# Eight pre-made weight sums and four more steps by seven products in the output projection of a gated linear attention block

## The chip, the cores and the metric

The kernel runs on one core of a Trainium2 chip. The metric is the device time of one execution in microseconds (us); the time of a kernel is the median over runs of the same build on the same chip. A traced execution is shown beside it: its span runs from the first to the last instruction of the trace.

## The reference

One layer of a streaming encoder, on 256 tokens of width 2048: a chunked gated linear attention (GLA) mixer and a squared-ReLU MLP, each behind an RMSNorm, and a last RMSNorm. All of it is float32.

```
def _gla_mixer(h, w_in, w_gate_up, b_gate, o_norm, w_out):
    q, k, v, r, g_low = jnp.split(h @ w_in, [...], axis=-1)
    log_a = log_sigmoid(g_low @ w_gate_up + b_gate) / 16
    ...
    def step(state, xs):                       # over chunks of 64 tokens
        state = d_c[..., None] * state + einsum('bhck,bhcv->bhkv', k_c, v_c)
        return state, einsum('bhck,bhkv->bhcv', q_c, state)
    ...
    o = o * rsqrt(mean(o * o) + EPS) * o_norm
    return (o * silu(r)) @ w_out

def _sq_relu_mlp(h, w_up, w_down):
    a = relu(h @ w_up)
    return (a * a) @ w_down

h = h + _gla_mixer(_rmsnorm(h, gla_norm), ...)
h = h + _sq_relu_mlp(_rmsnorm(h, mlp_norm), w_up, w_down)
return _rmsnorm(h, final_norm)
```

The change concerns `(o * silu(r)) @ w_out`, a product of 256 x 2048 by 2048 x 2048, and the part of the kernel ahead of it in which the projections of `h @ w_in` and the attention are computed (the mixer).

## The kernel before

**Splits.** Float32 accuracy is reached with float32r matmuls on parts. Each weight tile is loaded raw, ScalarE (ACT) casts it to `hi` (`copy_hi`, L118), and VectorE (DVE) subtracts to `lo` (`parts`, L131; `weights`, L165). A product then takes three matmuls on TensorE (PE): hi by hi, hi by lo, lo by hi. The hi and lo tiles come in five slots each, the raw tiles in six and one more named `more`. Loads of raw tiles are issued by SyncE (SP), a few by GpSimd (POOL).

**Stages.** In the order of the trace: warm-up matmuls (L252, `WARM` pairs of records), the first natural projection (the first half of V and the gate columns, `w_vg`), the gate's work, the turned projections of K and Q (`turned`, L206, matmuls at L219), and then three natural projections (`natural`, L178, matmuls at L176) of 16 steps each, one step per 128 rows of `w_in`: natural 2 (columns from 3*KEYW, the second half of V), natural 3 (from 4*KEYW) and natural 4 (from 5*KEYW), the two halves of the output gate r. After each step but the last, `pump` takes one closure off the queue `side` and runs it: two pairs of `scores` (L517, matmuls at L523, copies at L537 and L538) during natural 2, eight calls of `attend` (L563) during natural 3. An attend multiplies the scores by V, squares on ACT (L575), scales the sum on DVE (L576), raises it to the power -1/2 on POOL (L358) and scales the result on DVE (L579), which frees the PSUM bank. This stretch, from natural 2 to natural 4, is called the mixer below.

**Output projection.** `out_group` (L713) computes 512 of the 2048 output columns; there are four groups. Each takes eight steps, in the order given by `ORDER`, one for each pair of 128 rows of `w_out` (`kp`, 0 to 7). A step is done in one of two ways: plainly, with eight products of 128 x 256 by three matmuls, or by sums, with seven products after a scheme of 2 x 2 blocks, for the pairs in `FORMED`. For a step by sums, the left operand is turned into eight forms (`turn_pair`, L611, with `form_sums`), once for all groups; the weights' four blocks are combined for every group and pair: POOL adds two blocks during a load (L744, a DMA that accumulates), DVE makes the others (`weight_sums`, L603 to L605), ACT casts the four sums (L118) and DVE subtracts for their lo (L773). Three of the seven products use the raw blocks' splits, four the sums' (`pending`, L768).

**What sets the order.** The compiler of the kernel's framework lists each engine's instructions in one order, and each engine takes them in that order. `tc.issue_after` in the code puts an instruction behind a given one in that list. DMA queues belong to the engine that issues them. The MLP behind the output projection is not touched.

Of the kernel before, what the change touches and what calls it, by code (L numbers as in the profile page):

```python
# [60 lines left out]
EVEN = (5, 6)  # L61
MR = 2 * GT
ROUNDS = HID // MR
WARM = 8
FINE = 3


# [1 line left out]
def tile_gla_mlp(ctx, tc, x, xt, cols, w_vg, w_in, w_gate, w_out, w_up, w_down, final_norm, out):  # L69
# [33 lines left out]
    def flush():  # L103
        while side:
# [101 lines left out]
    def turned(row, w, c0, even=(0,), acc=None):  # L206

        acc = acc or acc_banks(GT // P // 2)
        for kp in range(KT // 2):
            wh, wl = pair_of(w, kp, c0, even)  # L210
            for i in range(2):
                kt = 2 * kp + i
                ah, al = row(kt)
                for j in range(GT // P):
                    s = slice(j * P, (j + 1) * P)
                    o = acc[j // 2][:, j % 2 * T : (j % 2 + 1) * T]
                    for n, (u, m) in enumerate(((wh, ah), (wh, al), (wl, ah))):
# [7 lines left out]
        return acc  # L225

    HALF = [(0, 512), (512, 1024)]

# [7 lines left out]
    def rows(w, c0, n=G, r0=0):  # L236
        return lambda kt: w[r0 + kt * P : r0 + (kt + 1) * P, c0 : c0 + n]
# [365 lines left out]
    def weight_sums(u):  # L603
        nc.vector.tensor_tensor(u[:, 2], u[:, 0], u[:, 2], op=ALU.subtract)  # L604
        return nc.vector.tensor_tensor(u[:, 1::2], u[:, 1::2], u[:, 2:3].to_broadcast([P, 2, T]), op=ALU.subtract)  # L605

    FORMED = (0, 1, 7)
    in_forms = lambda a: a.rearrange("p (f s) -> p f s", f=8)
    raw_forms = [in_forms(some[:, 4:6].rearrange("p a b -> p (a b)")), in_forms(mid.tile([P, G], F32, tag="db", name="form"))]

    def turn_pair(kp, bank, gain, to):  # L611

        raw_form = raw_forms[kp == 1]
# [38 lines left out]
    def forms_o(kp):  # L652
        if kp < 2:
            return [of_pairs[:, kp, i] for i in range(2)]
        return [a[:, OFF : OFF + G].rearrange("p (f s) -> p f s", f=8) for a in (oth, otl)]

    def place_o(kt):

# [47 lines left out]
    def then_mm():  # L706
# [3 lines left out]
            yield  # L710
        last_mm[0] = newest[0]

    def out_group(g, order, summed, between):  # L713

        tt = nc.vector.tensor_tensor
        banks = [out_banks[g, t] for t in range(NT)]
        sums_banks = []
        begun = set()
        pending = None
        block = lambda i, n=1: slice(i * T, (i + n) * T)  # L720

        def product(bank, o, a, w, n, last=False):
            for x in a[: 2 - n]:
                for d in range(0, w.shape[-1], T):
                    newest[0] = nc.tensor.matmul(  # L725
                        bank[:, o + d : o + d + T], x, w[:, d : d + T],
                        start=bank in sums_banks and bank.name not in begun, stop=last, skip_group_check=True,
                    ).ins
                    begun.add(bank.name)

        def products(these, w, last=False):
            with then_mm():
                for n in range(2):
                    for bank, o, a, c in these:
                        product(bank, o, a, w[n][:, c], n, last and n == 1)

        for step, kp in enumerate(order):
            by = kp in summed
            raw = raw_tile()[:, : 2 * GT]
            src = w_out[2 * kp * P : 2 * (kp + 1) * P, g * GT : (g + 1) * GT].rearrange("(i p) c -> p i c", p=P)  # L740
            if by:
                for i in range(2):
                    last_load[0] = nc.sync.dma_start(out=raw[:, i * GT : (i + 1) * GT], in_=src[:, i])
                nc.gpsimd.dma_start(out=raw[:, :T], in_=src[:, 0, T:], accum_op=ALU.add)  # L744
            else:
                last_load[0] = nc.sync.dma_start(out=raw.rearrange("p (i c) -> p i c", i=2), in_=src)
            w = parts(raw, 2 * GT, slots(), [(T * by, 2 * GT)])
            if by:
                if not sums_banks:
                    sums_banks.extend(psum_bank(i) for i in out_ids[4:])  # L750
                f = forms_o(kp)
                at = lambda k, f=f: [a[:, k] for a in f]
                p16, p57 = sums_banks
                products([(p16, 0, at(A11), block(1)), (banks[0], T, at(A12), block(3)), (banks[0], 0, at(S4), block(2))], w)
                u = raw.rearrange("p (f s) -> p f s", f=4)
                with tc.issue_after(last_lo[0].ins):
                    weight_sums(u)
            else:
                for t, i in ((0, 0), (0, 1), (1, 0), (1, 1)):
                    products([(banks[t], 0, row_o(2 * kp + i, t), block(2 * i, 2))], w, step == len(order) - 1 and i == 1)  # L760
            if pending:
                pending()
                pending = None
            if step in between:
                with tc.issue_after(last_hi[0].ins), tc.issue_after(last_lo[0].ins), then_mm():
                    between[step]()
            if by:
                def pending(u=raw, at=at, final=kp == [k for k in order if k in summed][-1]):  # L768
                    to = slots()
                    for a in range(2):  # L770
                        copy_hi(*(x.rearrange("p (f s) -> p f s", f=4)[:, a::2] for x in (to[0][:, :G], u)))
                    with tc.issue_after(last_lo[0].ins):
                        last_lo[0] = tt(to[1][:, :G], u, to[0][:, :G].bitcast(F32), op=ALU.subtract)  # L773
# [23 lines left out]
    out_group(0, ORDER, FORMED, {  # L797
        1: lambda: (turn(on, turned_o, gain_o, 2), turn(on, turned_o, gain_o, 3, forms_o, spare_out(0))),
        3: lambda: begin_out(1),
    })  # L800
    hth, htl = (big.tile([P, KT, T], F32R, tag="A" + i, name="h" + i, bufs=1) for i in "hl")
    turned_h = lambda kt: [a[:, kt, :].rearrange("p (t s) -> p t s", t=NT) for a in (hth, htl)]
    for g in range(1, GROUPS):
        out_group(g, ORDER, FORMED, {
            1: lambda: turn(h, turned_h, g2, g - 1), 4: lambda: ssq_h(g - 1),
            **({3: lambda: begin_out(g + 1)} if g + 1 < GROUPS else {}),
        })
# [511 lines left out]
```

## Time and profile before

| | us |
|---|---|
| median of three runs | 1043.82 |
| lowest and highest run | 1043.51, 1044.12 |
| the profiled execution: its time | 1043.33 |
| the profiled execution: its span | 1041.5 |
| first matmul of warm-up to the first projection | 1.05 to 4.77 |
| mixer (natural 2 to 4) | 139.8 to 286.7 |
| output projection | 286.7 to 374.4 |
| MLP | 374.4 to about 1032 |

The granted clock of TensorE is 0.999 of full speed over the execution. In the rows of the profile, a group's line number is that of the kernel before; PE is the matmul side of TensorE, PEld its weight loads; `xN` counts instructions, and a row of the timeline has start, length, engine, line, operation, output and inputs, and in brackets how long the engine was idle before it and what released it. A row of the chain of waits has start, length, engine, tile and line. Matmuls are pipelined: a record of 276 ns is followed by the next 113 ns later.

### The profile page before, as it was taken

The page shows a single profiled execution, that of the slowest core. Times are in us where ns is not written, and L with a number is a line of the kernel's source. Part 1 is how long each engine was busy: PE and PEld are TensorE (multiplying, and loading weights), DVE is VectorE, ACT ScalarE, POOL GpSimd, SP SyncE. Part 2 cuts the span into 40 slices and gives each one's busy share as a digit, 9 for nine tenths or more (in the row PEclk, how much of TensorE's full clock was granted, in tenths as well). Part 3 has the DMA queues.
Part 4 walks back from the last instruction along what each step waited for, and adds up shares of the span by engine and source line. Part 5 has one row for each costly group of instructions (what it writes and reads, how often), then busy time and mean ns, then how long its engine had stood idle before and what let it go on. Part 6 is the DMA issues. An engine that isn't in the chain of part 4 may idle for free.

```text
span 1041.5 us, 23180 instructions
## 1 busy us (share of the span) xinstructions
PE 1033.2 (99%) x9058; PEld 1032.8 (99%) x9058; DVE 865.3 (83%) x1171; ACT 736.9 (71%) x1088; POOL 119.5 (11%) x163
## 2 busy tenths in 40 slices
PE   9999999999999999999999999999999999999997
PEld 9999999999999999999999999999999999999997
DVE  6668654657599876989999999999999999999887
ACT  7685544546477665677778788778778778778685
POOL 0000000010111101111111121111111121111100
PEclk9999999999999999999999999999999999999999
DMA  9957664655667687678887887887888888887772
GB/s 341 338 164 220 189 199 144 181 145 180 194 182 210 206 263 197 175 207 239 224 249 226 230 233 227 233 243 214 253 227 225 245 228 228 237 233 219 234 243 86
DMA packets 119453, 226.79 MB, mean 218 GB/s; under 512 B 10752, under 2 KB 27904, under 8 KB 119216
## 3 DMA queue, kind: packets, MB, share of 16 engines
q1 hardware_dynamic: 100768, 207.46, 63.2%
q0 software_dynamic: 17856, 16.26, 10.3%
q10 hardware_dynamic: 720, 1.60, 0.4%
q8 instruction: 71, 1.16, 0.4%
q14 instruction: 38, 0.31, 0.1%
HBM read 223.17 MB, written 2.10 MB: 216 GB/s over the span
## 4 chain that ended last, share of the span: by engine, by line
PE 99%; issue 0%; ACT 0%; DVE 0%; POOLq 0%; POOL 0%; DVEq 0%
PE up L867 33%; PE acc L867 28%; PE acc L176 19%; PE acc L725 8%; PE acc L219 6%; PE aux L219 2%; PE aux L176 1%; PE aux L627 1%; PE aux L523 1%; PE aux L252 0%; ACT sqf L1206 0%; PE acc L424 0%; DVE hf L1278 0%; POOLq L1315 0%; POOL rf L358 0%
## 5 line engine op out<-in xcount | busy, mean ns | idle before, releaser
L118 ACT CAST hi<-raw 128x512 fp32r<-128x512 f32 (+4 forms) x634 | 512.0, 834 | 234.8 <-PE acc L176 69.0
L131 DVE TENSOR_TENSOR lo<-raw,hi 128x768 fp32r<-128x768 f32 (+3 forms) x226 | 238.0, 1057 | 100.1 <-ACT hi L118 97.4
L867 PE MATMUL acc<-hi,act 128*128 128x256 f32 x1696 | 247.7, 276 | 0.0
L867 PE MATMUL up<-hh,hi 128*128 128x256 f32 x1024 | 238.7, 276 | 0.0
L867 PE MATMUL up<-hl,hi 128*128 128x256 f32 x1024 | 238.7, 276 | 0.0
L165 DVE TENSOR_TENSOR lo<-raw,hi 128x1024 fp32r<-128x1024 f32 x160 | 194.7, 1219 | 28.3 <-ACT hi L118 26.3
L867 PEld LDWEIGHTS acc<-hi,act 128*128 128x128 f32 x1696 | 217.6, 188 | 0.0
L867 PEld LDWEIGHTS up<-hl,hi 128*128 128x128 f32 x1024 | 192.2, 188 | 0.0
L867 PEld LDWEIGHTS up<-hh,hi 128*128 128x128 f32 x1024 | 192.2, 188 | 0.0
L1077 POOL DMA_DIRECT2D raw<-in_w_down x112 | 97.1, 867 | 516.1 <-DMA raw<-in_w_down 231.0
L1137 DVE TENSOR_TENSOR lo<-raw,hi 128x1024 fp32r<-128x1024 f32 x112 | 136.4, 1218 | 1.1 <-ACT hi L118 1.1
L867 PE MATMUL up<-hh,lo 128*128 128x256 f32 x1024 | 137.0, 276 | 0.0
L867 PE MATMUL acc<-lo,act 128*128 128x256 f32 x848 | 133.8, 276 | 0.0
L867 PEld LDWEIGHTS up<-hh,lo 128*128 128x128 f32 x1024 | 125.7, 188 | 0.0
L867 PEld LDWEIGHTS acc<-lo,act 128*128 128x128 f32 x848 | 113.4, 188 | 0.0
L176 PE MATMUL acc<-hi,xA 128*128 128x256 f32 (+1 forms) x736 | 105.6, 278 | 0.0
L176 PEld LDWEIGHTS acc<-hi,xA 128*128 128x128 f32 x736 | 94.4, 188 | 0.0
L605 DVE TENSOR_TENSOR raw<-raw 128x512 f32<-128x512 f32 x124 | 85.6, 690 | 3.2
L176 PE MATMUL acc<-lo,xA 128*128 128x256 f32 (+1 forms) x368 | 61.5, 278 | 0.0
L604 DVE TENSOR_TENSOR raw<-raw 128x256 f32<-128x256 f32 x124 | 52.4, 423 | 2.9
L176 PEld LDWEIGHTS acc<-lo,xA 128*128 128x128 f32 x368 | 50.8, 188 | 0.2 <-DVE lo L131 0.2
L219 PE MATMUL acc<-xA,hi 128*128 128x256 f32 x288 | 49.2, 276 | 0.0
(181 smaller groups left out, 1220.0 us busy)
## 6 DMA issues: line engine op xcount, KB each, us to landing
raw<-in_w_up SPq DMA_DIRECT2D x128, 512.0 KB, 4.6
raw<-in_w_down SPq DMA_DIRECT2D x224, 256.0 KB, 4.3
raw<-in_w_in SPq DMA_DIRECT2D x80, 512.0 KB, 3.8
raw<-in_w_down POOLq DMA_DIRECT2D x112, 128.0 KB, 5.0
raw<-in_w_out SPq DMA_DIRECT2D x20, 512.0 KB, 4.9
raw<-in_w_down SPq DMA_DIRECT2D x16, 512.0 KB, 5.0
raw<-in_w_vg SPq DMA_DIRECT2D x14, 520.0 KB, 8.1
raw<-in_w_out SPq DMA_DIRECT2D x24, 256.0 KB, 3.5
```

The lines of the kernel that those rows point to most:

```text
L118: last_hi[0] = nc.scalar.copy(to, raw)
L131: last_lo[0] = nc.vector.tensor_tensor(lo[:, s], raw[:, s], hi[:, s].bitcast(F32), op=ALU.subtract)
L165: last_lo[0] = nc.vector.tensor_tensor(to[1], dst, to[0].bitcast(F32), op=ALU.subtract)
L176: nc.tensor.matmul(o[:, m], x, w[:, m], start=first and c == 0, stop=last, skip_group_check=True)
L219: nc.tensor.matmul(o, u[:, i, s], m, start=kt == 0 and n == 0 and j % 2 == 0, stop=kt == KT - 1 and n == 2, skip_group_check=True,)
L523: nc.tensor.matmul(o, kab[:, k[0], c0 + c, k[1] : k[1] + P], q(qt[:, c0 + c]), start=c == 0, stop=c == 1)
L604: nc.vector.tensor_tensor(u[:, 2], u[:, 0], u[:, 2], op=ALU.subtract)
L605: return nc.vector.tensor_tensor(u[:, 1::2], u[:, 1::2], u[:, 2:3].to_broadcast([P, 2, T]), op=ALU.subtract)
L725: newest[0] = nc.tensor.matmul(bank[:, o + d : o + d + T], x, w[:, d : d + T], start=bank in sums_banks and bank.name not in begun, stop=l ...
L867: newest[0] = nc.tensor.matmul(o, x, w, start=first, stop=last, skip_group_check=True).ins
L1077: nc.gpsimd.dma_start(out=raw[:, :T], in_=src[:, 0, T:], accum_op=ALU.add)
L1137: last_lo[0] = nc.vector.tensor_tensor(to[1][:, :G], u, to[0][:, :G].bitcast(F32), op=ALU.subtract)
```

## The change

Three things are edited. The warm-up count goes from 8 to 7. `FORMED` goes from (0, 1, 7) to (0, 1, 6, 7), so 16 of the output projection's 32 steps go by seven products where 12 did; the order of the pairs in a group is changed, with one order for the first group and one for the others. And for eight of these steps, listed in `MADE_OUT` as group and pair (three in group 1, three in group 2, two in group 3), the four weight sums and their hi and lo are made earlier: `make_all` is called ahead of natural 2, and fills a queue `jobs`, of which `pump` runs one after each step. For each of the eight there is a job that loads the pair's blocks with two POOL DMAs of 256 KB into the tile `more`, a job that does nothing, a job `high` that makes the sums on DVE and the hi on ACT into a hi/lo slot and stores it to DRAM by a POOL DMA of 512 KB, and a job `low` that makes the lo on DVE and stores it likewise; the next sum's load follows in the same job as `low`. In the output projection, such a step loads the raw blocks (without one that is not needed) and, by two SP DMAs of 512 KB, the ready hi and lo into one of two buffers (`pre`), and does no sums, cast or subtraction for them.

```
-WARM = 8
+WARM = 7
...
+    dram = ctx.enter_context(tc.tile_pool(name="dram", bufs=1, space=bass.MemoryType.DRAM))
...
-    side = deque()
+    side, jobs = deque(), deque()
...
                 if side:
                     side.popleft()()
+            if jobs:
+                jobs.popleft()()
...
+    MADE_OUT = ((1, 1), (1, 7), (1, 6), (2, 1), (2, 7), (2, 6), (3, 1), (3, 7))
+    made = {}
+
+    def make_sums(key, src):
+        made[key] = dram.tile([2, P, G], F32, tag=f"made{len(made)}", name="made")
+        raw, to = [], []
+
+        def load():
+            raw.append(wpool.tile([P, G], F32, tag="more", name="raw", bufs=1))
+            for i in range(2):
+                nc.gpsimd.dma_start(out=raw[0][:, i * GT : (i + 1) * GT], in_=src[:, i])
+
+        def high():
+            u = raw[0].rearrange("p (f s) -> p f s", f=4)
+            nc.vector.tensor_tensor(u[:, 0], u[:, 0], u[:, 1], op=ALU.add)
+            weight_sums(u)
+            to.extend(slots())
+            nc.scalar.copy(to[0][:, :G], raw[0])
+            nc.gpsimd.dma_start(out=made[key][0], in_=to[0][:, :G].bitcast(F32))
+
+        def low():
+            nc.vector.tensor_tensor(to[1][:, :G], raw[0], to[0][:, :G].bitcast(F32), op=ALU.subtract)
+            nc.gpsimd.dma_start(out=made[key][1], in_=to[1][:, :G].bitcast(F32))
+
+        return load, high, low
+
+    def make_all():
+        ...
+        for load, high, low in todo:
+            if jobs:
+                jobs[-1] = lambda then=load, first=jobs[-1]: (first(), then())
+            else:
+                jobs.append(load)
+            jobs.extend([lambda: None, high, low])
...
+    make_all()
     acc = natural(row_x, rows(w_in, 3 * KEYW), G, HALF, order=even_at(9, 11))
...
-    FORMED = (0, 1, 7)
+    FORMED = (0, 1, 6, 7)
...
             by = kp in summed
+            ready = made.get((None, g, kp))
...
-            if by:
+            if ready is not None:
+                if not made_o:
+                    made_o.extend(big.tile([P, 4 * G + 64], F32R, tag="C", name="pre")...)
+                ready_in = made_o[0]
+                made_o.reverse()
+                last_load[0] = nc.sync.dma_start(out=raw[:, T:GT], in_=src[:, 0, T:])
+                last_load[0] = nc.sync.dma_start(out=raw[:, GT:], in_=src[:, 1])
+                for i in range(2):
+                    last_load[0] = nc.sync.dma_start(out=ready_in[:, i].bitcast(F32), in_=ready[i])
+                ready = [ready_in[:, i] for i in range(2)]
+            elif by:
...
-                with tc.issue_after(last_lo[0].ins):
-                    weight_sums(u)
+                if not ready:
+                    with tc.issue_after(last_lo[0].ins):
+                        weight_sums(u)
...
-    ORDER = (3, 0, 2, 1, 4, 7, 5, 6)
+    ORDER = (3, 0, 2, 1, 4, 7, 6, 5), (0, 3, 2, 1, 7, 6, 4, 5)
```

More of the change, by code (lines that the diff above doesn't have):

```diff
@@ L225, in turned, with weight_sums @@
         return acc
+    def weight_sums(u):
+        nc.vector.tensor_tensor(u[:, 2], u[:, 0], u[:, 2], op=ALU.subtract)
+        return nc.vector.tensor_tensor(u[:, 1::2], u[:, 1::2], u[:, 2:3].to_broadcast([P, 2, T]), op=ALU.subtract)
+    MADE_OUT = ((1, 1), (1, 7), (1, 6), (2, 1), (2, 7), (2, 6), (3, 1), (3, 7))
+    MADE_DOWN = ()
+    made = {}
[18 more added lines that the diff above has]
+    def make_all():
+        pair = lambda w, c0, g: w[c0 : c0 + 2 * P, g * GT : (g + 1) * GT].rearrange("(i p) c -> p i c", p=P)
+        todo = [make_sums((None, g, kp), pair(w_out, 2 * kp * P, g)) for g, kp in MADE_OUT]
+        todo += [make_sums((ROUNDS - 1, g, kp), pair(w_down, (ROUNDS - 1) * MR + 2 * kp * P, g)) for g, kp in MADE_DOWN]
+        for load, high, low in todo:
[4 more added lines that the diff above has]
+            jobs.extend([lambda: None, high, low])
     HALF = [(0, 512), (512, 1024)]
@@ L611, in turn_pair @@
     def turn_pair(kp, bank, gain, to):
-        raw_form = raw_forms[kp == 1]
+        raw_form = raw_forms[kp % 2]
         for i in range(2):
@@ L654, in forms_o @@
             return [of_pairs[:, kp, i] for i in range(2)]
-        return [a[:, OFF : OFF + G].rearrange("p (f s) -> p f s", f=8) for a in (oth, otl)]
+        c = (12 * T + OFF + 128, OFF)[kp - 6]
+        return [in_forms(a[:, c : c + G]) for a in (oth, otl)]
     def place_o(kt):
@@ L711, in then_mm @@
         last_mm[0] = newest[0]
+    made_o = []
     def out_group(g, order, summed, between):
@@ L767, in out_group, with pending @@
             if by:
[L768 to L773, printed above, removed]
+                def pending(u=raw, at=at, final=kp == [k for k in order if k in summed][-1], to=ready):
+                    if not to:
+                        to = slots()
+                        for a in range(2):
+                            copy_hi(*(x.rearrange("p (f s) -> p f s", f=4)[:, a::2] for x in (to[0][:, :G], u)))
+                        with tc.issue_after(last_lo[0].ins):
+                            last_lo[0] = tt(to[1][:, :G], u, to[0][:, :G].bitcast(F32), op=ALU.subtract)
                     products([
@@ L792, in ssq_h @@
             nc.scalar.activation(sq, h[:, t, g * GT : (g + 1) * GT], AF.Square, accum_out=hs[:, t, g : g + 1])
-    ORDER = (3, 0, 2, 1, 4, 7, 5, 6)
+    ORDER = (3, 0, 2, 1, 4, 7, 6, 5), (0, 3, 2, 1, 7, 6, 4, 5)
     newest[0] = None
     ordered[0] = True
-    out_group(0, ORDER, FORMED, {
+    out_group(0, ORDER[0], FORMED, {
         1: lambda: (turn(on, turned_o, gain_o, 2), turn(on, turned_o, gain_o, 3, forms_o, spare_out(0))),
@@ L803, in tile_gla_mlp @@
     for g in range(1, GROUPS):
-        out_group(g, ORDER, FORMED, {
+        out_group(g, ORDER[1], FORMED, {
             1: lambda: turn(h, turned_h, g2, g - 1), 4: lambda: ssq_h(g - 1),
```

4 lines of the change are left out of this document (1 added, 3 removed).

## The prediction

> **What bounds the kernel now.** I read the page's first parts, then the waits of TensorE, then the chain of waits, then the busy time by stretches. The span of the profiled execution is 1041.5 us and its time 1043.33; the median of the runs, 1043.82, lies 0.49 above it.
>
> ```profile
> span 1041.5 us, 23180 instructions
> PE 1033.2 (99%) x9058; PEld 1032.8 (99%) x9058; DVE 865.3 (83%) x1171; ACT 736.9 (71%) x1088; POOL 119.5 (11%) x163
> ...
> PE aux L252 <- DVE ones L249: 1.1, 1, 1.1
> ...
> 139.80 24.48 PE acc L176 x216
> 164.28 3.08 PE aux L523 x24
> ...
> 195.83 2.72 PE acc L176 x24
> ...
> 292.23 20.82 PE acc L725 x183
> ```
>
> TensorE (PE) is busy 99% of the span, and the waits of PE (the third row) hold one entry, 1.1 us before the warm-ups. The chain is PE nearly throughout. So the only gain is matmuls left out, and any wait that PE gets is paid in full. One matmul costs 2.72/24 = 0.1133 us, and one step of the mixer's natural projections 2.72 us.
>
> ```profile
> 0.00:10.00 10.00, 8.95 (x62) 8.95 (x63) 4.31 (x10) 6.40 (x12) 1.77 (x9) 1.00 0.81 264
> 10.00:60.00 50.00, 49.99 (x418) 49.77 (x417) 35.98 (x48) 35.85 (x57) 1.07 (x2) 1.00 0.91 333
> ...
> 160.00:210.00 50.00, 50.00 (x435) 50.00 (x435) 28.94 (x43) 25.04 (x42) 2.19 (x4) 1.00 0.53 159
> 210.00:258.00 48.00, 48.00 (x425) 48.00 (x425) 28.95 (x40) 27.90 (x39) 2.19 (x4) 1.00 0.55 163
> 286.00:306.00 20.00, 20.00 (x179) 20.00 (x178) 18.78 (x28) 16.35 (x26) 1.75 (x2) 1.00 0.52 149
> 306.00:330.00 24.00, 24.00 (x214) 24.00 (x213) 22.42 (x31) 18.33 (x31) 3.08 (x4) 1.00 0.78 237
> ```
>
> Columns: stretch, length, busy PE, weight loads, DVE, ACT, POOL, granted clock, DMA share, GB/s. The start is full of DMA (0.91 of the engines from 10 to 60 us). The mixer (140 to 286 us) has room: DVE busy 28.94 of 50, ACT 25.04, DMA 0.53. The output projection has little on DVE: 18.78 of 20.
>
> **The gain.** Four more of the 32 steps go by seven products instead of eight, three matmuls each: 12 x 0.1133 = 1.36 us in L725's stage. The warm-up that is left out is worth nothing:
>
> ```profile
> 9.10 1.06 ACT L118 CAST hi<-raw 128x1040 fp32r<-128x1040 f32 x1 [0.70 <-DMA raw<-in_w_vg]
> ...
> 10.19 1.24 DVE L131 TENSOR_TENSOR lo<-raw,hi 128x1040 fp32r<-128x1040 f32 x1 [1.06 <-ACT hi L118]
> ...
> 11.49 0.41 PEld L176 LDWEIGHTS acc<-lo,xA 128*128 128x128 f32 x3 [0.23 <-DVE lo L131]
> ...
> raw<-in_w_vg SPq DMA_DIRECT2D x14, 520.0 KB, 8.1
> ```
>
> At 11.49 us PE already waits 0.23 us for a split that follows its load at once (load landed 9.10, cast, subtraction to 11.43). A PE that starts earlier waits longer there. Bounds 0 to the 3.72/16 x 2 = 0.46 us of two warm-up matmuls, whose chain row is here; I take 0.
>
> ```profile
> 1.05 3.72 PE aux L252 x16
> ```
>
> **The start.** The first of the eight sums' loads waits for nothing, and in the compiled order it stands right behind POOL's set-up, so it runs in the first microseconds, not in the mixer: 2 x 256 KB = 0.52 MB through the same 16 engines as the loads that PE waits for. At 333 GB/s that is 1.6 us of DMA; with the lateness already 0.23 us it has no cover. Lower bound 0 (it fills holes, the first 10 us being 0.81 used), upper 1.6. I take 1.3, because the row it is nearest to is the full stretch.
>
> **The mixer.** What covers a delay there is the lead of the splits:
>
> ```profile
> 148.00 1.05 ACT L118 CAST hi<-raw 128x1024 fp32r<-128x1024 f32 x1 [1.66 <-PE acc L176]
> ...
> 149.08 1.22 DVE L131 TENSOR_TENSOR lo<-raw,hi 128x1024 fp32r<-128x1024 f32 x1 [1.49 <-ACT hi L118]
> ```
>
> Steps start at 139.80 + 2.72k. The cast at 148.00 was released by PE's end of the third step (five hi/lo slots), so it is for the eighth, at 158.84: lead 9.8 us for hi, 8.5 for lo. A sum now takes one of the five slots, and its cast and subtraction stand in the in-order queues of ACT and DVE ahead of the next weights' own. So the next weights wait for the whole chain of the sum:
>
> ```profile
> L744 POOL DMA_DIRECT2D raw<-in_w_out x12: 872/874/1033, 268.4 to 351.0; - x12
> ...
> DMA to landing us min/median/max: 3.1/5.2/6.4
> L604 DVE TENSOR_TENSOR raw<-raw 128x256 f32<-128x256 f32 x124 | 52.4, 423 | 2.9
> L605 DVE TENSOR_TENSOR raw<-raw 128x512 f32<-128x512 f32 x124 | 85.6, 690 | 3.2
> ```
>
> POOL issues the store of the former lo and two loads (3 x 0.87), and the last lands 3.1 to 5.2 us after its issue began: 4.8 to 6.9 us. DVE's two adds and the double one take 0.42 + 0.42 + 0.69 = 1.5 us; then ACT casts the sum and then the weights (2 x 1.05), DVE makes the weights' lo and the sum's (2 x 1.22), and the next cycle begins. That is 10.8 to 12.9 us a cycle, against three steps of 2.72 = 8.2 us of PE (some 9.5 with scores and attends between). Each cycle eats 1.3 to 3.4 us of the lead, so within three or four of the seven cycles it is gone.
>
> The Trainium skill ("DMA: Bandwidth & Descriptors", section "Anatomy of one DMA — SWDGE (gpsimd) path") gives such a transfer about 2.0 us plus its bytes at 436 GB/s, an estimate of 2.6 us for 256 KB, less than the 3.1 us that the row shows at the least for half the bytes. By the page the cycle would be some 10.3 us, the loads would never be late, and the sum below would lose about 1 us.
>
> With the lead gone, what decides is what stands in front of a sum in the queues. In the compiled order the scores and the attends come before sums, whose casts come before the weights that PE needs at once. An attend's chain:
>
> ```profile
> 200.00 0.69 ACT L575 ACTIVATE sq<-aux,r1k 128x512 f32<-128x512 f32 x1 [0.37 <-PE aux L176]
> 200.59 0.19 ACT L575 ACTIVATION_READ_ACCUMULATOR sq<-aux,r1k 128x1 f32 x1
> ...
> 200.81 0.15 DVE L576 TENSOR_SCALAR oss<-oss 128x1 f32<-128x1 f32 x1
> 201.63 0.81 DVE L579 TENSOR_SCALAR on<-aux,r1k,ors 128x512 f32<-128x512 f32 x1 [0.67 <-POOL ors L358]
> ```
>
> From PE's end of an attend to the row of 0.15 us is 1.0 us, and to the end of the last 2.5. The places, each counted from PE's last cover:
>
> - Natural 3 (the columns at 4*KEYW), tenth step: PE has the last attend and then this step. ACT has that attend's square, the eighth sum's cast, the step's cast; the sum's double add stands on DVE behind the attend's 0.15 us operation. 1.0 + 0.69 + 1.05 + 1.05 = 3.8 us, with three hand-overs between engines of about 0.1 us; the step's lo (1.22) is then wanted after four matmuls (0.45), another 0.8. Sum 4.5 us.
> - The same stage, seventh step: 1.0 + 0.42 + 0.69 + 1.05 + 1.05 + 0.3 = 4.5 us behind the first of three attends that PE takes in a row, less the other two, (12 + 6) x 0.1133 = 2.0. 2.5 us.
> - Natural 2 (3*KEYW), thirteenth step: the fourth sum stands behind the second scores' casts and adds:
>
> ```profile
> 176.65 0.65 ACT L537 ACTIVATE at<-aux,r 64x64 fp32r<-64x64 f32 x2 [0.22 <-DVE at L538]
> ...
> 176.99 0.62 DVE L538 SCALAR_TENSOR_TENSOR at<-aux,r,at 64x64 fp32r<-64x64 f32 x2 [0.19 <-ACT at L537]
> ```
>
> From the scores' last matmul to these adds' end some 0.9 us, then 0.69 + 1.05 + 1.05: 3.7 us, less the eleven matmuls that PE has left, 1.25. 2.4 us.
> - Its last step and the fourth of the next stage: lateness of the load against the cycle, 1.3 us each (0.5 to 2.2 by the ends of the landing row).
>
> Together 4.5 + 2.5 + 2.4 + 2.6 = 12 us. Low end: only the first three, each less 1 us of lead that is left: 6.4. High end: every one of seven cycles short by 2.4 (12.9 less 9.5 and one more hand-over), 17 us. The transfers themselves fit: 12.6 MB more (8 x 0.5 loaded, 8 x 1 stored) in some 80 us is 157 GB/s beside 159; the share goes from 0.53 to about 1.0, so it just about closes, which is why I take the landing's median and not its minimum. POOL's own work for the attends, the step between the 0.15 and the 0.81 us rows above, now stands behind stores and loads of 0.87 us each; the tenth step's place bears it, as its sum is the last one.
>
> **The output projection.** Made steps load 1 MB of ready splits through SP instead of forming and splitting on DVE and ACT. In the first group nothing is made, but four steps go by sums, and the forms of a fourth pair are turned: about 3.3 us more of DVE (0.42 + 0.69 for the sums, 1.2 for their split, about 1.0 for the forms, by the same rows) where 18.78 of 20 us are busy. Idle there is 1.2, so up to 2.1 us of PE; nothing, if the lead covers it. Groups two and three draw 2 x 1 MB and more each: the stretch that has 237 GB/s at 0.78 now comes near 0.95. A buffer is free only when PE ends the step before last, some 45 matmuls = 5.1 us ahead, about the landing of such a load:
>
> ```profile
> raw<-in_w_out SPq DMA_DIRECT2D x20, 512.0 KB, 4.9
> ```
>
> Bounds 0 and 4 us; I take 0.7, since the groups behind the first lose DVE work (2.3 us a made step) at the same time.
>
> **Sum.** 1043.33 - 1.36 + 1.3 + 12 + 0.7 = 1056.0 us.
>
> **Rivals.**
> - *The jobs stay hidden* (the other side). The place is the mixer; the price is only the gain. It holds if the loads land in less than about 3 us, so that a cycle needs no more than the 9.5 us that PE spends, and if the lead of 8.5 us then bears the 3.8 us chains. For it: DVE and ACT have 21 and 25 us free in the 50 shown. Against it: queues are in order, so free time behind a waiting instruction is no use, and the compiled order puts it there. Time 1043.33 - 1.36 = 1042.0; with 1.3 at the start 1043.3. Faster than the measurement can tell (0.2%, 2.1 us) would need the warm-up and more on top.
> - *Half of it*: the lead does not run out in natural 2, and PE pays only the two places in natural 3, 7.0 us. 1043.33 - 1.36 + 1.3 + 7.0 = 1050.3. For it: the last attends come in the second half, and the lead at 148 us is long.
> - *The loads rule*: with DMA near 1.0 each landing goes to its 6.4 us maximum and the mixer costs 17 to 19. Time about 1062.
> - *The clock falls* in the 4.5 us gap: the granted clock is 1.00 in all rows, since PE never idles. At half clock one natural step costs 2.72 us more, so 1056 + 2.7 = 1058.7. The Trainium skill ("TensorE: Matmul & The Clock Gate", Part 1) says that an idle window of about 3.4 us halves the clock until PE has been busy as long; no row here can show it.
> - *The output projection is bound by loads or DVE* while the mixer is hidden: 1043.33 - 1.36 + 1.3 + 4 = 1047.3.
>
> **How the numbers follow.** Forecast 0.55, within 1052 to 1061; half of it 0.17; loads rule 0.07; the clock 0.06; the projection alone 0.04; hidden 0.11, of which 0.03 faster by over 0.2% and 0.08 within it. Slower 0.89. Range: from 1046, which leaves out the hidden case, to 1063, which holds the loads. Time 1056.
>
> **What would show it.** Right: waits of PE on the casts and subtractions of weights between 165 and 240 us, longest at the tenth step of natural 3 (3.5 to 4.5 us); the first stage longer by about 1.3; 720 product matmuls in the output projection instead of 4 x 183 = 732; DMA near 1.0 in the mixer. Wrong: no PE wait over 1 us in the mixer, or waits for DMA alone, or a wait of PE in the output projection larger than in the mixer.

## The result, and the profile after

The changed kernel takes 1079.43 us (median of four runs, 1076.66 to 1080.06) against 1043.83 for the kernel before: ratio 1.0336, 95% interval 1.0317 to 1.0355. It is slower, as forecast, but by 35.6 us where the forecast said 12, and outside the range of 1046 to 1063.

The stages, each from its first matmul record to that of the next, in us of the profiled execution (1080.06 us, span 1078.1):

| stage | before | after | difference | predicted |
|---|---|---|---|---|
| up to natural 2 | 139.64 | 142.17 | +2.53 | +1.3 |
| mixer (natural 2 to 4) | 146.93 | 177.10 | +30.17 | +12 |
| output projection | 87.65 | 91.77 | +4.12 | -0.66 |
| MLP and end | 667.29 | 667.03 | -0.26 | 0 |

The page's totals, the waits of PE (waiter, what it waited for, us in total, times, the longest), and the busy time by the stretches that were shown of before:

```profile
span 1078.1 us, 23270 instructions
PE 1048.0 (97%) x9044; PEld 1043.4 (97%) x9044; DVE 876.7 (81%) x1193; ACT 737.5 (68%) x1089; POOL 135.7 (13%) x191
```

```profile
PE acc L179 <- ACT hi L121: 16.3, 9, 4.7
PE aux L179 <- DVE on L627: 2.4, 1, 2.4
PE acc L772 <- DMA pre<-made: 1.8, 2, 1.0
PE aux L671 <- DVE h L847: 1.2, 1, 1.2
PE aux L299 <- DVE ones L296: 1.1, 1, 1.1
```

```profile
160.00:210.00 50.00, 39.68 (x299) 38.88 (x298) 25.98 (x42) 19.19 (x33) 7.71 (x15) 0.90 0.63 204
210.00:258.00 48.00, 40.88 (x305) 39.72 (x304) 30.90 (x43) 21.06 (x32) 12.21 (x19) 0.89 0.64 217
...
341.00:363.00 22.00, 19.98 (x169) 19.34 (x169) 18.01 (x25) 15.06 (x25) 0.89 (x1) 1.00 0.87 283
363.00:385.00 22.00, 21.00 (x182) 20.80 (x181) 14.35 (x21) 13.55 (x22) 1.75 (x2) 1.00 0.89 309
```

Where there was one wait there are five kinds. Of the first two rows 17.4 us lie in the mixer, on the weights' casts (L121 is `copy_hi`) and behind an attend, as forecast; the other 1.3 us are three waits for casts in the first 11 us. Two things stand beside them that the sum did not hold. The granted clock is 0.90 and 0.89 in the mixer. And DMA is at 0.63 over the stretch, not near 1.0; what it is while a sum's load is in flight is shown under e4_loslot.

One cycle of a made sum, from POOL's, DVE's and ACT's timelines of the changed kernel and its row of PE:

```profile
160.77 0.54 POOL L259 DMA_DIRECT2D made<-lo  x1 [2.80 <-DVE lo L258]
161.31 1.09 POOL L247 DMA_DIRECT2D raw<-in_w_out  x2
173.68 0.54 POOL L255 DMA_DIRECT2D made<-hi  x1 [11.29 <-ACT hi L254]
177.02 0.54 POOL L259 DMA_DIRECT2D made<-lo  x1 [2.80 <-DVE lo L258]
```

```profile
169.67 0.43 DVE L251 TENSOR_TENSOR raw<-raw 128x256 f32<-128x256 f32 x1 [6.93 <-DMA raw<-in_w_out]
171.11 0.43 DVE L231 TENSOR_TENSOR raw<-raw 128x256 f32<-128x256 f32 x1 [1.01 <-DMA raw<-in_w_out]
171.57 0.69 DVE L232 TENSOR_TENSOR raw<-raw 128x512 f32<-128x512 f32 x1
...
172.34 1.04 ACT L254 CAST hi<-raw 128x1024 fp32r<-128x1024 f32 x1 [12.36 <-DVE raw L232]
173.29 2.93 ACT L121 CAST hi<-raw 128x1024 fp32r<-128x1024 f32 x3
...
174.38 0.75 PE L179 MATMUL acc<-hi,xe_gt 128*128 128x256 f32 x4 [4.38 <-ACT hi L121]
```

The lo store goes out at 160.77, the next sum's two loads behind it at 161.31, and DVE gets the second block only at 171.11, more than nine us later. ACT stands idle 12.36 us in front of the sum's cast, with three casts of weights queued behind it, and PE waits 4.38 us for the first of them. From one lo store to the next are 16.25 us. Over all eight sums the hi stores run from 142.15 to 250.45 us: 108.3 / 7 = 15.5 us a cycle.

### The profile page after: what moved, and what is told of

Read it like the earlier page. It is cut to its first block, busy times and chain, and to the rows that moved or that the text cites. A ratio compares the mean times of both kernels' runs of the same rounds, so it can differ in the third digit from the quotient of the medians.

```text
span 1078.1 us, 23270 instructions
## 1 busy us (share of the span) xinstructions
PE 1048.0 (97%) x9044; PEld 1043.4 (97%) x9044; DVE 876.7 (81%) x1193; ACT 737.5 (68%) x1089; POOL 135.7 (13%) x191
## 4 chain that ended last, share of the span: by engine, by line
PE 87%; issue 6%; DMA 3%; POOL 1%; ACT 1%; DVE 1%; SPq 0%; POOLq 0%; DVEq 0%; ACTq 0%
PE up L927 32%; PE acc L927 27%; PE acc L179 12%; PE acc L772 7%; PE acc L222 6%; PE aux L222 2%; DMA pre<-made 1%; DMA raw<-in_w_out 1%; DMA raw<-in_w_vg 1%; PE aux L671 1%; POOL raw L247 0%; ACT hi L121 0%; POOL made L255 0%; POOL made L259 0%; DVE raw L232 0%
## 5 line engine op out<-in xcount | busy, mean ns | idle before, releaser
L121 ACT CAST hi<-raw 128x768 fp32r<-128x768 f32 (+4 forms) x626 | 504.5, 835 | 204.3 <-DVE raw L231 64.6
L179 PE MATMUL acc<-hi,xA 128*128 128x256 f32 (+1 forms) x736 | 110.1, 285 | 6.1 <-ACT hi L121 6.1
L179 PEld LDWEIGHTS acc<-hi,xA 128*128 128x128 f32 x736 | 98.1, 193 | 7.7 <-ACT hi L121 7.7
L232 DVE TENSOR_TENSOR raw<-raw 128x512 f32<-128x512 f32 x128 | 88.4, 691 | 3.4
L179 PE MATMUL acc<-lo,xA 128*128 128x256 f32 (+1 forms) x368 | 65.0, 288 | 0.1
L179 PEld LDWEIGHTS acc<-lo,xA 128*128 128x128 f32 x368 | 53.4, 195 | 0.9 <-DVE lo L134 0.7
```

Source lines behind the costliest of these rows:

```text
L121: last_hi[0] = nc.scalar.copy(to, raw)
L179: nc.tensor.matmul(o[:, m], x, w[:, m], start=first and c == 0, stop=last, skip_group_check=True)
```

## The experiments

Stages in us of each profiled execution. The time is a median for the kernel before, the changed one (four runs each), e8, e9 and e12 (10, 11 and 11 runs), and one run for the rest; the kernel before, run beside them, took 1043.84 to 1043.92 (medians).

| kernel | to natural 2 | mixer | output projection | time |
|---|---|---|---|---|
| before | 139.64 | 146.93 | 87.65 | 1043.83 |
| changed | 142.17 | 177.10 | 91.77 | 1079.43 |
| e1_formed | 140.19 | 146.94 | 88.05 | 1044.02 |
| e2_late | 140.09 | 175.59 | 89.17 | 1073.75 |
| e3_nolo | 141.60 | 165.52 | 90.90 | 1067.17 |
| e4_loslot | 140.06 | 155.27 | 91.22 | 1055.61 |
| e5_spread | 140.23 | 149.16 | 90.78 | 1049.33 |
| e6_turn2 | 140.05 | 146.93 | 90.31 | 1046.52 |
| e7_hold | 139.70 | 166.39 | 90.96 | 1066.29 |
| e8_warm7 | 140.29 | 146.94 | 87.64 | 1043.52 |
| e9_three | 139.97 | 146.94 | 87.02 | 1043.43 |
| e10_fill | 141.95 | 174.15 | 90.31 | 1075.32 |
| e11_five | 139.89 | 147.40 | 86.62 | 1043.48 |
| e12_five | 140.07 | 147.40 | 86.63 | 1043.95 |

### e1_formed: four more steps by sums, nothing made ahead

```
-    MADE_OUT = ((1, 1), (1, 7), (1, 6), (2, 1), (2, 7), (2, 6), (3, 1), (3, 7))
+    MADE_OUT = ()
```

> The changed kernel with an empty list of sums to make ahead: nothing is made in the mixer, sixteen steps by seven products all form their sums in place, seven warm-ups. If the mixer's jobs and the ready loads carry the loss: mixer back to 147 us (139.8 to 286.7), first projection's wait back to about 11.5 us, output projection 87.65 - 1.36 plus what DVE cannot hide (0 to 3 us), time 1042 to 1045. If the order of the steps or the four more steps by sums carry a part of it: output projection over 90 us, time above 1046.

1044.02 us, the mixer back to 146.94 to the hundredth. So the mixer's whole loss is the jobs'. The output projection is 0.40 us longer than before in spite of 12 matmuls less, with one wait in it:

```profile
PE aux L671 <- DVE h L847: 1.2, 1, 1.2
```

This is the start of the turning of the first group's finished columns, which waits for DVE's last add there. DVE is busy 21.52 of the group's 22 us (windows of e1_formed), 20.62 before in the same 22 us. The fourth step by sums is too much for that group, and the wait takes back what the matmuls gave.

### e2_late: the first load out of the start

```
+            with tc.issue_after(last_pow[0].ins):      # behind the token norm's power on POOL
                 for i in range(2):
                     nc.gpsimd.dma_start(...)
```

> The changed kernel with the first sum's load put behind the token norm's power on POOL, out of the first microseconds; nothing else. If that load is what delays the first projection (14.03 us against 11.49 for the matmuls behind the third weight's lo): back to about 11.5 us and the time 2.5 us lower, about 1077. If the missing warm-up is the cause, nothing moves there: 14.0 us and 1079.

Natural 2 begins at 140.09 instead of 142.17. The executions without an early load (before, e1, e2, e4 to e9, e11) lie between 139.64 and 140.29 there, with eight warm-ups or seven; so the load costs about 2 us, and 139.64 was the low end. In the chain of the changed kernel one sees what it does, the load that the third weight's split waits for:

```profile
4.01 7.60 DMA raw<-in_w_vg
11.62 0.02 issue
11.64 1.07 ACT hi L121
```

Issued at 4.0 us as before, it lands at 11.62 instead of 9.10. The time fell by more than this, 5.7 us against the median: the mixer came out 1.5 and the output projection 2.6 us shorter. In e2_late's waits of PE the two for ready splits (1.8 us in the changed kernel) are missing; why was not tried.

### e8_warm7: one warm-up less, alone

```
-WARM = 8
+WARM = 7
```

> The kernel before with seven warm-ups instead of eight, nothing else. My prediction: nothing, 0 to -0.46 us, since PE waits for a split behind its load at 11.5 us anyway. If a shorter warm-up lets the first matmuls run at half clock: up to 0.5 us slower.

Ratio 0.9998, interval 0.9988 to 1.0007: nothing, as predicted.

### e3_nolo: no store of the lo

```
         def low():
             nc.vector.tensor_tensor(to[1][:, :G], raw[0], to[0][:, :G].bitcast(F32), op=ALU.subtract)
-            nc.gpsimd.dma_start(out=made[key][1], in_=to[1][:, :G].bitcast(F32))
...
-                    ... dma_start(out=ready_in[:, i].bitcast(F32), in_=ready[i])
+                    ... dma_start(out=ready_in[:, i].bitcast(F32), in_=ready[0])
```

> The changed kernel without the store of the sums' lo; the ready steps read the hi twice, so that part of the output's sums is left out. If a sum's load lands late because it stands behind that store in POOL's queue: landings of the loads from 7.0 us median to 4 to 5, a cycle of the sums from 15.7 us to about 12, mixer from 177 us to 155 to 165, time 1058 to 1068. If the DMA engines are short: an eighth of the traffic of that stretch gone, landings 6 us, time about 1074. If the order of the casts on ACT and DVE alone decides: no change, 1078.

The mixer falls by 11.6 us to 165.5, just past the end of the first theory's range, and the time to 1067.17. The landings of the sums' loads (minimum, median, maximum) fall less than that theory said:

```profile
DMA to landing us min/median/max: 4.5/6.3/8.2
```

Nor is it the hi store, which is issued 3.3 us or more ahead of the loads, for it has landed by then (in one cycle 0.2 us later). These are its landings in e3_nolo:

```profile
DMA to landing us min/median/max: 2.9/2.9/3.5
```

The sums' hi stores run from 141.58 to 238.19 us, 13.8 us a cycle instead of 15.5. So the lo store costs about 1.7 us a cycle, which is the 11.6 us over seven cycles; but with no store in front a load still needs 6.3 us, where 4 to 5 were expected.

### e4_loslot: loads in front of the stores

```
-            u = raw[0].rearrange("p (f s) -> p f s", f=4)
-            nc.vector.tensor_tensor(u[:, 0], u[:, 0], u[:, 1], op=ALU.add)
-            weight_sums(u)
             to.extend(slots())
-            nc.scalar.copy(to[0][:, :G], raw[0])
+            u, v = (... for a in (raw[0], to[1][:, :G].bitcast(F32)))     # sums go to the lo slot
+            nc.vector.tensor_tensor(v[:, 0], u[:, 0], u[:, 1], op=ALU.add)
+            ...
+            then()                                                        # the next sum's loads
+            nc.scalar.copy(to[0][:, :G], to[1][:, :G].bitcast(F32))
+            with tc.issue_after(last_job[0].ins):                         # stores behind them
```

> The changed kernel with the sums made into the lo slot instead of in place, so that the raw tile is free at once and the next sum's loads are issued a whole cycle ahead, in front of the stores; the first load late as in the run above. If the loads' lateness is what PE pays: mixer loss of 30 us falls to 0 to 5, no half clock, time 1043 to 1050. If the sums' place in the queues of ACT and DVE behind scores and attends is enough for a loss (my prediction's second part): three to four waits of PE of 2 to 4.5 us stay, mixer loss 8 to 14 us and more with the clock, time 1052 to 1062.

The mixer loses 8.3 us instead of 30.2. That is at the low end of the second theory, though with one wait of over 1 us where it had three to four. The edit does two things for a load: it is issued before the sum's cast and lo, so that its landing no longer stands in line with them, and it goes out in front of their stores. Here are the landings of the sums' loads, first of the changed kernel, then of this one, and then the stretch of 160 to 190 us of the two in the same order:

```profile
DMA to landing us min/median/max: 5.3/7.0/9.2
```

```profile
DMA to landing us min/median/max: 3.7/4.5/5.3
```

```profile
160.00:190.00 30.00, 24.43 (x190) 24.04 (x189) 14.11 (x27) 10.22 (x20) 4.34 (x8) 0.94 0.58 193
```

```profile
160.00:190.00 30.00, 30.00 (x255) 30.00 (x254) 22.45 (x35) 16.87 (x29) 4.93 (x9) 1.00 0.90 313
```

With a DMA share of 0.90 and 313 GB/s the loads land in 4.5 us; with 0.58 and 193 GB/s they took 7.0. These shares are means of 30 us, however. From a pair's first issue to its last landing the engines are as busy in the changed kernel (0.72 to 0.95 over the seven pairs) and in e3_nolo (0.72 to 0.99) as in this one (0.70 to 1.01). One such stretch of each, in this order:

```profile
161.31:171.02 9.71, 8.69 (x74) 8.50 (x72) 1.86 (x3) 0.00 (x0) 1.08 (x3) 1.00 0.72 251
157.25:166.03 8.78, 8.78 (x80) 8.78 (x79) 2.40 (x3) 0.00 (x0) 1.06 (x2) 1.00 0.74 229
167.03:172.40 5.37, 5.37 (x48) 5.37 (x48) 3.64 (x6) 3.90 (x8) 2.20 (x4) 1.00 1.00 366
```

So busy engines alone do not make a load late, for with 1.00 the last one landed in 4.8 us; and the lo store is only a part, as e3_nolo shows. One more thing differs. In the changed kernel and in e3_nolo the casts of three weights stand together behind the sum's, their raw tiles come free together, and SP issues three loads of 512 KB around each pair, here with the pairs of 161.31 and 157.25:

```profile
159.37 3.74 SPq L171 DMA_DIRECT2D raw<-in_w_in  x3
155.85 3.73 SPq L171 DMA_DIRECT2D raw<-in_w_in  x3
```

In those two runs, two loads of weights are issued within 2.6 us behind each pair's first load; in e4_loslot, the next one is issued about 3 us behind it or later. No run changes that alone, so how the rest of the lateness divides between the store and the loads of weights is open. What the runs show is the worth of e4_loslot's edit as a whole: 20.3 of the 28.7 us that the mixer loses in e2_late.

The longest wait that is left in e4 is 2.8 us, in front of the last attend, as its timelines show:

```profile
223.41 0.43 DVE L254 TENSOR_TENSOR lo<-raw 128x256 f32<-128x256 f32 x1 [3.69 <-DMA raw<-in_w_out]
...
225.18 0.21 DVE L628 TENSOR_SCALAR oss<-oss 128x1 f32<-128x1 f32 x2
...
226.94 0.80 PE L180 MATMUL aux<-vh,at 128*128 128x256 f32 x2 [2.81 <-DVE on L631]
```

DVE waits 3.69 us for a sum's load with two attends' small operations behind it, their bank is not freed, and PE cannot begin the last attend, ahead of the tenth step of natural 3. It is the order of the queues that the prediction spoke of, but the other way round: there the sum stood behind the attend, here the attends stand behind the sum.

### e5_spread and e7_hold: no job beside an attend

```
-            if jobs:
+            if jobs and not (side and hold[0]):        # hold: during natural 3
```

e5_spread is this edit on e4_loslot, e7_hold on e2_late.

> Sums made in the lo slot with early loads, as in e4_loslot, and none of the jobs run while attends are in the side queue: five sums in natural 2, one at the end of natural 3, two in natural 4. If what is left of the mixer's loss there (8.3 us) comes from sums standing before attends in DVE's and ACT's queues: mixer 147 to 149 us, half clock gone, time 1047 to 1049 (the rest in the output projection). If it comes from the load on DVE, ACT and DMA as a whole: 153 to 156 us, time 1053 to 1056.

> The changed kernel's own jobs (sums in place, load behind the lo store) with the first load late, and no job while attends are in the side queue. If the loads' chain of 15 us a sum is the main loss wherever it stands: natural 2 keeps its waits (4.4 and 1.2 us and half clock, some 9 us), natural 4 gets new ones, mixer 156 to 170 us, time 1055 to 1068. If the attends are the main loss: mixer 147 to 152 us, time below 1052.

e5: mixer 149.16, 1049.33 us, just past the first theory's ends; its one wait there is 1.5 us, early in natural 4, for ACT's work on natural 3's result. e7: mixer 166.39, with natural 2's waits much as they were (3.1, 1.2 and 5.1 us) and new ones of 0.9 and 1.8 in natural 4. So of the 28.7 us that the mixer loses in e2_late, early loads take away 20.3 (e4), and keeping off the attends 6.1 more (e5), which leaves 2.2; the latter alone takes away 9.2 (e7) and leaves the chain of loads.

### e10_fill: work of zeros in the waits

```
+            for i in range(fill.get(step, 0)):
+                nc.tensor.matmul(acc[i % 2][0][:32, :T], none, prev[:, :T], start=False, stop=False, ...)
...
-    acc = natural(..., order=even_at(9, 11))
+    acc = natural(..., order=even_at(9, 11), fill={11: 34, 15: 36})
```

and {6: 18, 9: 28} in natural 3; `none` is a tile of zeros.

> The changed kernel with matmuls by a tile of zeros, added to the running sums, ahead of the four steps that PE waits longest for (34, 36, 18 and 28 of them, 3.9, 4.1, 2.0 and 3.2 us, a little less than the waits of 4.4, 4.7, 2.4 and 3.8 us): work that changes nothing in the sums, put where PE is idle, so that its clock should stay. If the 8.3 us that the mixer's matmuls spend at the doubled spacing of 0.213 us add to the time: no matmuls at 0.213 us, time lower by 6 to 9 us, 1070 to 1073. If they stand beside the chain of the sums' loads, which sets the pace until 234 us: the waits only move, time lower by 1 to 4 us, 1075 to 1078. If the zeros do not count as activity or delay the steps: the same or slower, 1079 to 1085.

The question was the clock. In the changed kernel, behind each long wait the matmuls of the timeline stand 0.213 us apart instead of 0.113:

```profile
174.96 1.03 PE L179 MATMUL acc<-hi,xA 128*128 128x256 f32 x4
...
180.28 0.63 PE L179 MATMUL acc<-hi,xA 128*128 128x256 f32 x4
```

Four records take 1.03 us there and 0.63 us five us later. Summed over the mixer's records (each spacing between 0.16 and 0.32 us, less 0.113, less what the scores have of such spacings before), that is 8.3 us. With the zeros the same sum is 3.5 us and the waits of over 0.32 us are 8.4 us instead of 19.7, yet the mixer is only 2.95 us shorter, 174.15. The first 34 zeros stood in a wrong place: the wait of 4.38 us is the tenth step's, and they stand in front of the twelfth, so that 2.8 us of this wait and the half clock behind it stayed. The sums' hi stores run from 141.93 to 249.53, 107.6 us instead of 108.3. Up to the tenth step of natural 3, where the chain of loads ends, the zeros took away 2.5 us of doubled spacing, and the time fell by 0.7; behind it they took away 2.3, and the time fell by 2.2. So beside the chain of loads the half clock was hidden for the most part, since a faster PE waits longer at the next sum, and behind the chain it was paid. The middle theory holds.

### e6_turn2, e9_three, e11_five, e12_five: a version that beats both?

e6_turn2 is e1_formed with eight warm-ups and the turn of the finished columns a step later; e9_three instead keeps the first group at three steps by sums, in the order of before:

```
-            1: lambda: turn(h, turned_h, g2, g - 1), 4: ...
+            2: lambda: turn(h, turned_h, g2, g - 1), 4: ...
```

```
-    out_group(0, ORDER[0], FORMED, {
+    out_group(0, ORDER[0], (0, 1, 7), {
```

> No sums made ahead, eight warm-ups, sixteen steps by seven products, and the turning of the finished columns one step later (after the third step of groups 2 to 4). If the one wait of 1.2 us in e1_formed (PE for DVE's last add of group 1's columns) is all that eats the 1.36 us: it goes, output projection 86.5 to 87.0 us, time 1042.5 to 1043.2, faster than before by 0.7 to 1.3 us. If DVE's load is what limits: the wait moves to a later step, time 1043.5 to 1044.2.

> No sums made ahead, eight warm-ups, the first group by three steps of seven products as before, the other three groups by four (15 steps): nine matmuls less than before. In e1_formed the only wait of the output projection is 1.35 us, PE for the last add of the first group, whose DVE is overloaded by the fourth step by sums. If that is right: the wait goes, output projection 87.65 - 1.02 = 86.6 us, time 1042.8, faster than before by 0.8 to 1.1 us. If DVE cannot bear four steps in any group (97% busy there): waits of 0.5 to 2 us in groups 2 to 4, time 1043.3 to 1045.

e6 missed: the wait went over to a lo split (1.1 us) and small waits add to it, output projection 90.31, 1046.52 us. e9 has no wait left in its output projection, which is 0.63 us shorter, but in the MLP 0.46 us of that are lost again up to the first turn's end (from its first matmul at 373.93 to the next long row at 387.41 are 13.48 us, 13.02 before). Ratio 0.9994, interval 0.9985 to 1.0003: the 0.8 to 1.1 us that were expected cannot be told. Five of its eleven runs took 1041.96 to 1042.29 and the other six 1043.43 to 1044.97, against 1043.23 to 1044.24 for the kernel before; what parts the two groups is not known.

e11_five takes e5_spread, that first group, eight warm-ups and five sums, none for pair 6:

```
-    MADE_OUT = ((1, 1), (1, 7), (1, 6), (2, 1), (2, 7), (2, 6), (3, 1), (3, 7))
+    MADE_OUT = ((1, 1), (1, 7), (2, 1), (2, 7), (3, 1))
```

> As e5_spread (sums into the lo slot, early loads, none beside attends), with five sums instead of eight, none of them for pair 6, and the first group by three steps as before; fifteen steps by seven products. All five are made in natural 2. If a ready step costs PE only where its buffer comes free late (pair 6, waits of 1.2 and 1.4 us in the changed kernel): mixer 147 to 148.5, output projection 86.6 to 87.2, time 1043 to 1045. If the larger traffic of ready steps costs more than that: output projection 88 us and above, time 1045 to 1047.

> The kernel of e11_five once more, timed: PE has no wait in its trace behind the first projection, its mixer is 0.47 us longer than before and its output projection 1.03 us shorter. If that holds in all runs: 0.3 to 0.8 us faster than before, ratio 0.9993 to 0.9997. If the first look was chance: ratio 0.9997 to 1.0005, no difference that can be told.

All five sums are made in natural 2 with PE waiting nowhere behind the first projection; its waits are again one row:

```profile
PE aux L303 <- DVE ones L300: 1.1, 1, 1.1
```

The output projection is 86.62, 1.03 us less than before, as nine matmuls fewer would make it, and the mixer 147.40. e12_five is the same kernel timed: ratio 1.0000, interval 0.9991 to 1.0009. The 0.56 us that its stages show lie below what a run can tell. No version here is shown to be faster than the kernel before.

## Why the prediction was right in direction and too small

**The gain and the warm-up.** Right. The stage has 12 matmuls less, 1.36 us, and e8 shows nothing for the warm-up.

**The start.** Right in place and mechanism, too small: 1.3 predicted, about 2 measured (2.53 against the one execution of before), over the upper bound of 1.6. That bound was bytes over bandwidth; a load of 520 KB that is on its way through the same engines was held back longer than that. Why was not tried.

**The mixer.** This is the step that failed, and in it one term: "the last lands 3.1 to 5.2 us after its issue began". The loads took 5.3 to 9.2 us to landing. With the issues ahead of it the prediction had 4.8 to 6.9 us from the start of the lo store to the last landing; in the cycle shown above DVE gets the block after 10.3 us (160.77 to 171.11), and over the seven cycles the landings come 8.0 to 10.3 us behind that start. The rest of the chain was sized rightly: from there to the next lo store are 5.9 us (171.11 to 177.02) against 1.5 + 2.1 + 2.44 = 6.0. So the cycle became 15.5 us instead of 10.8 to 12.9. The row that gave the term was of transfers of 128 KB with no store ahead of them, in another stage. I listed the lo store and priced its issuing, 0.87 us, but not its transfer; by e3 the store is worth 1.7 us a cycle. What makes the rest of the landing so long, the loads of weights that are issued with the sum's or something else, stays open. What PE needed for the same work can be read off the two chains, by the row of 240 matmuls that begins with the tenth step of natural 3, before and after:

```profile
222.35 27.20 PE acc L176 x240
```

```profile
251.15 31.10 PE acc L179 x240
```

Before, that step comes 222.35 - 139.80 = 82.6 us after natural 2 begins, or 11.8 us for each of the seven cycles, lead included. 7 x (15.5 - 11.8) = 26 us; it comes 28.8 us later, 2.5 of them from the start. The remaining 3.9 us (31.10 - 27.20) come behind the last sum, at half clock for the most part. With the cycle of 10.8 to 12.9 that the prediction had, the same reckoning gives -7 to +8 us: the 12 came from places and not from this chain. The high end of 17 us was also summed wrongly, for 12.9 less 9.5 is 3.4 and not 2.4; seven times that is 23.8.

**The places.** The waits of PE came nearly where they were forecast, their sizes mostly not. The tenth step of natural 3: 3.76 us against 3.8 for the hi, along the chain that was listed:

```profile
247.51 0.69 ACT L623 ACTIVATE sq<-aux,r1k 128x512 f32<-128x512 f32 x1 [8.75 <-PE aux L179]
247.78 0.42 DVE L231 TENSOR_TENSOR raw<-raw 128x256 f32<-128x256 f32 x1 [1.76 <-DMA raw<-in_w_out]
...
248.32 0.15 DVE L624 TENSOR_SCALAR oss<-oss 128x1 f32<-128x1 f32 x1
248.39 0.68 DVE L232 TENSOR_TENSOR raw<-raw 128x512 f32<-128x512 f32 x1
...
249.11 1.04 ACT L254 CAST hi<-raw 128x1024 fp32r<-128x1024 f32 x1 [0.82 <-DVE raw L232]
...
250.06 2.93 ACT L121 CAST hi<-raw 128x1024 fp32r<-128x1024 f32 x3
...
251.15 1.43 PE L179 MATMUL acc<-hi,xA 128*128 128x256 f32 x5 [3.76 <-ACT hi L121]
```

That the number fits is luck in part. The second row shows that the sum's load came late as well: DVE was done with its add at 248.20, 0.2 us before the listed chain let it go on, so the load alone would have cost nearly the same wait; and in e2_late the same step waits 5.5 us. The seventh step: 2.4 + 0.3 us against 2.5, but the 2.4 are a wait for the bank of an attend (DVE's `on`) and not for a cast. The thirteenth of natural 2: 1.2 against 2.4. Its last: 4.7 against 1.3, the fourth of natural 3: 0.6 against 1.3, and the tenth of natural 2, not forecast, 4.4, which waits for a cast behind a late load, as the last does. These waits add to 17 us, and the mixer lost 30. Of the difference 8.3 us are doubled spacings of matmuls, and the rest lies in other spacings; but to add waits and spacings up, as one does from a trace, does not tell what the clock costs, because PE spent at half clock a part of the time that it would else have waited (e10).

**DMA.** "About 1.0" was wrong for the stretch: 0.63 and 0.64, and 0.72 to 0.95 while a pair of loads is in flight. The sums' traffic came, but spread over 30 us more.

**The output projection.** +4.12 where 0.7 less 1.36 was forecast. Three waits, all at places that were named, and all larger: the first group's DVE (1.35 us beyond a matmul's spacing, also in e1 without any ready step), and the ready splits of pair 6 in the second and third group (1.8 us in two, by the page's waits); the rest lies in smaller spacings. In these groups DVE has 4 and 7.7 us of 22 free and DMA is at 0.87 to 0.89: the saved work was not what limited. Without pair 6 and with three steps in the first group, in e11, all of it is gone.

**The rivals.** "The loads rule" came nearest, 1062 us and chance 0.07; its landings were even past the 6.4 us it allowed, at a share of 0.72 to 0.95 and not 1.0 while they were in flight. "The clock falls" came true as an event and was priced at 2.7 us; e10, which took away 4.8 of the 8.3 us of doubled spacing, gained 3. The Trainium skill ("TensorE: Matmul & The Clock Gate", Part 1) gives about 3.4 us of idling as the window behind which the clock halves. The trace agrees on the halving, but in e4 the wait of 2.81 us above was enough for 3.2 us of matmuls at 0.214 us.

## What to carry to other kernels

A price for a transfer holds for its place and its company: the loads that were priced at 3.1 to 5.2 us took 5.3 to 9.2 behind a 512 KB store and among three loads of weights. So put the next load in front of the stores, out of line with the work on the last one, and give it a buffer that does not wait for them; here that took away 20 of 29 us. Work that is moved into a stretch with free time should be costed as a chain (load, add, cast, store, back to the next load) against the steps that PE takes meanwhile, and not as busy time against idle time: here DVE and ACT had 42 and 50% of the stretch free, and 30 us were lost. And a saving of 1.4 us under an engine that is 94 to 98% busy is only there if that engine's own work does not grow in the same group.

## What was not expected of the hardware

A pair of 256 KB loads was landed 5.4 us after its first issue with the DMA engines 1.00 busy meanwhile (e4), and after 8.8 us with 0.74 and no store in front of it (e3); why is open. Behind waits of PE of 2.4 to 2.8 us the matmuls stood 0.213 us apart for 2.9 to 3.5 us, in the changed kernel, e3, e4 and e10, and in e7 behind one of 1.8 us, which ends at 266.13; the granted clock of the stretch that follows, third from the end of its row, is 0.50:

```profile
266.83:270.24 3.41, 3.41 (x18) 3.38 (x17) 3.41 (x4) 3.41 (x7) 0.54 (x1) 0.50 0.82 271
```

Behind one of 2.3 (e2) and another of 2.6 us (e3) they did not, nor behind any of 1.5 us and less.
